# Attention's waits for tiles and banks: query turns in a projection bank, products moved ahead of a head's first turn, and the second key/value projection's banks in another order

## The chip, the cores and the metric

The kernel runs on one core of one Trainium2 chip. The metric is the device time of one execution in microseconds (us); less is better. Three runs of the kernel before gave 2050.15, 2051.71 and 2051.81 us, a median of 2051.71 us.

## The reference

One encoder layer is computed for two inputs of 512 tokens x 1024 channels, x_prompt (sample 0, s = 0 in the code) and x_sample (s = 1), with the same weights. Cut to what matters:

```python
x = x + 0.5 * swiglu(rms_norm(x, ffn1_norm), ffn1_w_gate, ffn1_w_up, ffn1_w_down)
h = rms_norm(x, mix_norm)
aq, ak, av, mq, mk, mv, gate_pre, o_pre, g_att, g_mlstm = split(h @ w_in)
aq = rope(rms_norm(heads(aq), q_norm))            # 8 query heads of 64
ak = rope(rms_norm(heads(ak), k_norm))            # 2 key/value heads
att = softmax(aq @ ak.T * 64 ** -0.5) @ av        # over all 512 keys
mem = mlstm_bidirectional(mq, mk, mv, gate_pre)   # 4 heads of 128, both directions
merged = sigmoid(g_att) * (att @ w_up_att) + sigmoid(g_mlstm) * (mem @ w_up_mlstm)
x = x + merged @ w_out
x = x + 0.5 * swiglu(rms_norm(x, ffn2_norm), ffn2_w_gate, ffn2_w_up, ffn2_w_down)
return rms_norm(x, final_norm)
```

Everything is float32, to float32 accuracy.

## The kernel before

**Precision.** A float32 operand is split into a rounded high part (written by ScalarE, L715) and the rest (VectorE, L716); a product is then three matmuls, high x high, high x rest, rest x high, summed in PSUM. In the profile they read `xh,w` and `xl,w`. Transposes are matmuls with the identity (`ident`).

**Order of the work.** Both samples' first feed-forward block, then for each sample `mix` (L840), a generator that holds the attention, the mLSTM and the merge, then the second feed-forward block. TensorE (PE) runs what is issued in program order where the code pins it (`pin`); VectorE (DVE) and ScalarE (ACT) are ordered by a scheduler, from the places of their instructions in the program and from what these wait for.

**PSUM.** It has eight banks of 128 x 512 floats. In `mix` they come from four pools, each of which hands its banks out in turn and makes the next user wait until the last reader of that bank is done: MM has three (tiles `mm`, for projections), PS two (`pss`, for scores), PT two (`pst`, for transposes), PO one (`pso`, for the products with the values).

**The projections of `mix`.** `tok_proj` (L783, matmuls on L800) computes keys, values and gates of all 512 tokens into four banks at once, 272 columns each: for each of eight slices of the weights, twelve products, three for each bank in turn. Its banks are listed by the caller: (PS, PS, MM, MM). In the second sample the merge of the first stands just ahead: `merge_mem` writes its last banks from PS and PT in turn, and VectorE reads each on L1218 (`scalar_tensor_tensor`). `proj` (L808) is a projection of 128 columns, 24 products into one bank of MM, that can be had as single steps (L820); its result is read by gates on ScalarE and VectorE.

**Gates.** `gates` (L948) sums the logarithms of the forget gates with two triangular matrices for each direction and with a matrix of ones (L970), products of 16 columns.

**Attention** (from L1150). A head h has four blocks b of 128 queries. `score(h, b)` makes a bank of scores (two products, L1091), VectorE takes the row maximum (L1094), ScalarE the exponential and its sum (L1096), VectorE the reciprocal (L1097), and the tile is scaled: on ScalarE (L1099) for odd b in the first sample, save head 0's last, else on VectorE (L1101). The values are wanted with the keys on the partitions, so `turn_keys(Ps, b)` (L1107) transposes 128 columns of **all four** tiles of a head into a bank of PT, and L715/L716 split it. `values` (L1118) multiplies the split tile of the turn before. So the loop of one (h, b) is: a query pair's turn, if it is due; score(h+1, b); five product steps of the projections; turn(h, b); three steps; values of the turn before. `among(n)` takes n such steps, out of a queue of projections for the attention gate and the output gate; they run out in head 6. Ahead of the loop the four scores of head 0 are made, with nine steps after each (`FIRST`).

The queries are turned in pairs of heads: `q_turn(pr)` (L1038) transposes four blocks into a bank of PT (`pair_turn`, L900), and four copies, two on ScalarE (L1041) and two on VectorE (L1042), take it to `qT`. Pair 0 is turned ahead of the loop, pairs 1 to 3 inside it, at h = 0, 2, 4 and b = 2.

Of the kernel before, what the change touches and what calls it, by code (L numbers as in the profile page):

```python
# [16 lines left out]
P = 128  # L17
# [9 lines left out]
def encoder(ctx, tc, I, outs):  # L27
    nc = tc.nc
# [13 lines left out]
    def nm(s):  # L42
        n_id[0] += 1
        return f"{s}_{n_id[0]}"
# [71 lines left out]
    def PT():  # L116
        return pt.tile([P, S], F32, tag="t", name=nm("pst"))

    def f(ap):
        return ap.bitcast(F32)  # L120
# [7 lines left out]
    ones = cpool.tile([P, P], F32, name="ones")  # L128
# [157 lines left out]
    def load_w(view, key, park=True):  # L286


        if key in parked:
            d, shape = parked[key]  # L290
            w2 = wpool.tile(shape, F32R, tag="w8", bufs=4, name=nm("w"))
            for i in range(2):
                nc.sync.dma_start(f(w2[:, i]), d[:, i])
            return w2[:, 0], w2[:, 1]
        raw = fetch_w(view)
        with shifted(-WEIGHTS):
            hi, lo = split_w(raw, V_)
        if not park:
            return hi, lo
        shape = [P, 2] + list(raw.shape[1:])  # L300
        parked[key] = d, _ = dpool.tile(shape, F32, name=nm("wpark")), shape
        for i, t in enumerate((hi, lo)):
            nc.sync.dma_start(d[:, i], f(t))
        return hi, lo
# [424 lines left out]
    tabs = []  # L729
# [41 lines left out]
    def go(*units):  # L771
        for load, comp in units:
            held.append((comp, load()))
            while len(held) > ahead[0]:
                c, w = held.pop(0)
                c(w)
# [6 lines left out]
    def tok_proj(xh, xl, cols, kk, done, banks):  # L783

        N = sum(n for _, n in cols)
        p = []

        def load(k0):
            return load_w([win_v[:, k0:k0 + kk, c:c + n] for c, n in cols], ("in", cols[0], k0))

        def comp(k0, w):
            wh, wl = w
            if not p:
                p.extend(b() for b in banks)
            for kl in range(kk):
                k = k0 + kl
                for b in range(4):
                    bs = slice(b * P, (b + 1) * P)
                    for i, (a, w_) in enumerate(((xh, wh), (xh, wl), (xl, wh))):
                        nc.tensor.matmul(p[b][:, :N], a[:, k, bs], w_[:, kl, :],  # L800
                                         start=(k == 0 and i == 0), stop=(k == KD - 1 and i == 2))
            if k0 + kk == KD:
                done(p)

        return [(lambda k0=k0: load(k0), lambda w, k0=k0: comp(k0, w)) for k0 in range(0, KD, kk)]
# [29 lines left out]

    OUT = 3
    FILLER = 5,3
    FIRST = 9

    def mix(s, xh, xl, early=None, extra=None, after=None):  # L840

# [8 lines left out]
        def F2(dtype=F32):  # L850
            return T2(dtype, "f2")
# [42 lines left out]
            yield tt(v, v, cg.unsqueeze(2).to_broadcast([P, 4, 2, DA]), op=ALU.mult)  # L894
            yield tt(v, v, m, op=ALU.add)

        def pair_turn(o, keep):
            p = PT()
            for b in range(4):
                keep(nc.tensor.transpose(p[:, b * P:(b + 1) * P], o[:, b, :], ident))  # L900
            return p
# [17 lines left out]
        qraw, rq = mg[:, 4:8, :], []  # L919
# [18 lines left out]
        def gs(tag):  # L938
            t = small(32, tag)
            return t, t.rearrange("p (d b h) -> p d b h", d=2, b=4)  # L940
# [7 lines left out]
        def gates():  # L948
            Gb = Gt.rearrange("p (b c) -> p b c", b=4)
            V_.tensor_tensor(Gb, Gb, gbias.unsqueeze(1).to_broadcast([P, 4, 16]), op=ALU.add)  # L950
            Gv = Gt.rearrange("p (b d g h) -> p b d g h", b=4, d=2, g=2)

            Fs, Fv = gs("Fs")
            Is, Iv = gs("Is")
            for dst, g in ((Fv, 1), (Iv, 0)):
                G_.tensor_copy(dst[:, 0], Gv[:, :, 0, g, :])
                for b in range(4):
                    G_.tensor_copy(dst[:, 1, 3 - b], Gv[:, b, 1, g, :])
            fa, _ = gs("fa")
            V_.scalar_tensor_tensor(fa, Fs, -1.0, Fs, op0=ALU.mult, op1=ALU.min)  # L960
            nc.scalar.activation(fa, fa, AF.Exp)
            nc.scalar.activation(fa, fa, AF.Ln, bias=1.0)
            nc.scalar.activation(warm, fa[:, 0:1], AF.Exp)
            Lt, _ = gs("Lt")
            V_.scalar_tensor_tensor(Lt, Fs, 0.0, fa, op0=ALU.min, op1=ALU.subtract)
            p = PT()
            for d in range(2):
                rhs = Lt[:, d * 16:(d + 1) * 16]
                for j, lhs in enumerate((tabs[2][:, 2 * d, :], tabs[2][:, 2 * d + 1, :], ones)):
                    nc.tensor.matmul(p[:, j * 32 + d * 16:j * 32 + (d + 1) * 16], lhs, rhs, start=True, stop=True)  # L970
            V_.tensor_copy(cs, p[:, 0:96])
            et, ev = gs("fa")
            V_.tensor_tensor(et, Is, cs[:, 32:64], op=ALU.add)
            p = PT()
            nc.tensor.transpose(p[0:32, 0:P], et, ident)
            rows = F2()[0:32]
            er, run = rows[:, 0:P], rows[:, P:2 * P]
            V_.tensor_copy(er, p[0:32, 0:P])
            nc.sync.dma_start(ebuf.rearrange("d b h s -> (d b h) s"), er)
            V_.tensor_tensor_scan(run[:, ::-1], er[:, ::-1], er[:, ::-1], NEG, op0=ALU.max, op1=ALU.max)  # L980
            V_.tensor_tensor_scan(run[0:16], er[0:16], er[0:16], NEG, op0=ALU.max, op1=ALU.max)
            top = rows[:, 2 * P:2 * P + 1]
            V_.tensor_reduce(top, er, axis=AX.X, op=ALU.max)
            return run, top

        def gate_tops(run, top):
            p = PT()
            pin(nc.tensor.transpose(p[:, 0:32], run, ident[0:32, 0:32]))
            pin(nc.tensor.transpose(p[:, 32:64], top.to_broadcast([32, P]), ident[0:32, 0:32]))
            V_.tensor_copy(st[:, 0:2], p[:, 0:64].rearrange("p (i d b h) -> p i d b h", i=2, d=2, b=4))  # L990
# [44 lines left out]
        def q_rope(pr):  # L1035
            return rope_steps(qraw[:, :, pr * P:(pr + 1) * P], rq[0][:, :, 2 * pr:2 * pr + 2], tabs[0])

        def q_turn(pr, keep):  # L1038
            p = pair_turn(qraw[:, :, pr * P:(pr + 1) * P], keep)
            for h, own, other in ((2 * pr, lower, upper), (2 * pr + 1, upper, lower)):  # L1040
                nc.scalar.activation(qT[own, h, :], p[own, :], AF.Copy)  # L1041
                V_.tensor_tensor(qT[other, h, :], p[own, :], f(qT[own, h, :]), op=ALU.subtract)  # L1042

        go(*tok_proj(xh, xl, [(512, 256), (2304, 16)], 2, kv_done, (PS, PS, MM, MM)))
        if early:
            early()
        go(*tok_proj(xh, xl, [(0, 512)], 2, q_done, (MM, PO, MM, MM)), mem_qk(0, 0), mem_qk(0, 1))
# [3 lines left out]
        with shifted(60):  # L1051
            k_turn()
            q_turn(0, lambda i: i)
# [82 lines left out]
        def among(n):  # L1136
            for _ in range(n):
                if not between:
                    if not held:
                        return  # L1140
                    c, w = held.pop(0)
                    if queue:
                        load, c2 = queue.pop(0)
                        held.append((c2, load()))
                    between.extend(c.steps(w))
                between.pop(0)()
# [6 lines left out]
        for b in range(4):  # L1153
            Ps.append(score(0, b))
            next(rope, None)
            among(FIRST)
        last = None
        for h in range(HA):
            nxt = []
            for b in range(4):  # L1160
                if h in (0, 2, 4) and b == 2:
                    q_turn(h // 2 + 1, pin)
                if (h, b) == (0, 1):
                    gate_tops(*tops)
                if (h, b) in ((0, 3), (2, 3)):
                    rope = q_rope(h // 2 + 2)
                if h < 4:
                    next(rope, None)
                if h + 1 < HA:
                    nxt.append(score(h + 1, b))  # L1170
                among(FILLER[0])
                pp = turn_keys(Ps, b)
                among(FILLER[1])
                if last:
                    values(*last)
                last = h, b, pp
                if extra and b == 2 and h in (2, 3, 4):
                    extra[h - 2]()
            Ps = nxt
# [320 lines left out]
    def keep(k, eng=None):  # L1500
        pin(keep_x(0, k, banks[k], x0r[k], eng))
# [156 lines left out]
    def mid_parts(s):  # L1658
# [10 lines left out]
        return one, two, three  # L1669

    m0 = mix(0, *nhl[0], None, mid_parts(1), prep1)
    for _ in range(3):
        next(m0)
# [182 lines left out]
```

## Time and profile before

| | |
|---|---|
| median of three runs | 2051.71 us (2050.15 to 2051.81) |
| the profiled execution's own time | 2048.82 us |
| its span | 2047.0 us |
| granted TensorE clock in it | 0.999 |
| instructions | 26767 |
| PE, matmuls (x9317) | 2033.1 us busy |
| VectorE (x2780) | 1571.5 us busy |
| ScalarE (x1655) | 909.0 us busy |
| GpSimd (x116) | 93.4 us busy |
| DMA | 445.38 MB, mean 218 GB/s |

The profile is that of one execution. A row of the timeline gives the start and the length in us, the engine, the line of the kernel, the operation, output tile <- input tiles, shape and type, and xN where N instructions alike stand together (the length is then from the first one's start to the last one's end). In brackets stands how long the engine had been idle before it and what ended that. PE's matmuls overlap: the next starts before the one ahead has ended, so PE's distance from start to start is shorter than the length of one. The waits of PE give, for each kind of instruction, what it waited for: us in total, times, longest.

### The profile page before, as it was taken

The numbers are of one execution on the slowest core, as the hardware profiler recorded it, in microseconds if no ns is written. First come the engines' busy times: TensorE is split into PE (matmuls) and PEld (weight loads), VectorE is DVE, ScalarE is ACT, GpSimd is POOL, SyncE is SP. The second block draws the span as 40 slices with busy tenths as digits, with TensorE's granted clock in tenths as the row PEclk, the third lists the DMA queues.
The fourth block names the chain that finished last, engine by engine and source line by source line (L and its number), as shares of the span: only waits on it lengthen the run. The fifth ranks groups of instructions, "written<-read, shape, count | busy, mean of one in ns | idle before, by whom it ended". The sixth has DMA issues, their size and how long they took to land.

```text
span 2047.0 us, 26767 instructions
## 1 busy us (share of the span) xinstructions
PE 2033.1 (99%) x9317; PEld 1679.9 (82%) x9317; DVE 1571.5 (77%) x2780; ACT 909.0 (44%) x1655; POOL 93.4 (5%) x116
## 2 busy tenths in 40 slices
PE   9999999999999999999999999999999999999998
PEld 7888888888888878888888888888888888888887
DVE  8888888886797888776567756366788988786797
ACT  7544444443234567563324554134544444442224
POOL 0000000001003000100120000001000000000001
PEclk9999999999999999999999999999999999999999
DMA  9656566799766853868564345667655655599753
GB/s 316 199 168 226 174 203 194 240 339 357 262 224 225 292 164 128 286 212 289 187 190 137 117 150 174 221 202 228 193 186 184 197 175 183 198 345 347 272 200 119
DMA packets 314727, 445.38 MB, mean 218 GB/s; under 512 B 19848, under 2 KB 189920, under 8 KB 313312
## 3 DMA queue, kind: packets, MB, share of 16 engines
q1 hardware_dynamic: 312512, 437.69, 63.8%
q0 software_dynamic: 1920, 5.72, 0.9%
q8 instruction: 73, 1.20, 0.2%
q14 instruction: 62, 0.51, 0.1%
q10 hardware_dynamic: 160, 0.27, 0.0%
HBM read 284.06 MB, written 159.55 MB: 217 GB/s over the span
## 4 chain that ended last, share of the span: by engine, by line
PE 95%; DVE 3%; ACT 1%; DMA 0%; issue 0%; SPq 0%; DVEq 0%; ACTq 0%
PE mm L833 16%; PE pst L374 12%; PE pso L374 12%; PE mm L374 11%; PE mm L632 8%; PE pss L374 6%; PE pst L632 4%; PE pss L632 4%; PE mm L820 4%; PE mm L800 4%; PE pso L632 3%; PE pso L1118 1%; PE pst L1107 1%; PE pss L1091 1%; PE pso L1287 1%; PE pss L1237 1%
## 5 line engine op out<-in xcount | busy, mean ns | idle before, releaser
L374 PE MATMUL pst<-xc,w 128*128 128x512 f32 x1056 | 253.7, 389 | 0.0
L374 PEld LDWEIGHTS pst<-xc,w 128*128 128x128 f32 x1056 | 198.3, 188 | 41.1
L374 PE MATMUL mm<-xc,w 128*128 128x512 f32 x972 | 229.4, 390 | 0.0
L374 PEld LDWEIGHTS mm<-xc,w 128*128 128x128 f32 x972 | 182.0, 188 | 37.7 <-ACT f L382 0.2
L632 PE MATMUL mm<-rt,w 128*128 128x512 f32 x765 | 178.7, 389 | 0.0
L833 PE MATMUL mm<-xh,w 128*128 128x512 f32 x560 | 176.9, 392 | 0.0
L632 PEld LDWEIGHTS mm<-rt,w 128*128 128x128 f32 x765 | 143.5, 188 | 29.7
L332 ACT ACTIVATE w<-t 128x512 fp32r<-128x512 f32 x176 | 106.6, 627 | 135.5 <-issue 63.1
L333 DVE TENSOR_TENSOR w<-t,w 128x512 fp32r<-128x512 f32 x176 | 117.8, 688 | 42.5 <-ACT w L332 41.0
L374 PE MATMUL pso<-xc,f 128*128 128x512 f32 x528 | 126.8, 389 | 0.0
L374 PE MATMUL pss<-xc,w 128*128 128x512 f32 x528 | 126.8, 389 | 0.0
L374 PE MATMUL pso<-xc,w 128*128 128x512 f32 x528 | 126.8, 389 | 0.0
L833 PEld LDWEIGHTS mm<-xh,w 128*128 128x128 f32 x560 | 104.9, 188 | 21.8
L374 PEld LDWEIGHTS pss<-xc,w 128*128 128x128 f32 x528 | 99.1, 188 | 20.6
L374 PEld LDWEIGHTS pso<-xc,w 128*128 128x128 f32 x528 | 99.1, 188 | 20.5
L374 PEld LDWEIGHTS pso<-xc,f 128*128 128x128 f32 x528 | 99.1, 188 | 20.6
L820 PE MATMUL mm<-xh,w 128*128 128x512 f32 x336 | 114.5, 401 | 0.0
L833 PE MATMUL mm<-xl,w 128*128 128x512 f32 x280 | 109.6, 391 | 0.0
L715 ACT ACTIVATE w<-wr 128x512 fp32r<-128x512 f32 x72 | 45.1, 632 | 136.7 <-PE pso L632 70.7
L278 ACT ACTIVATE w<-wr 128x1024 fp32r<-128x1024 f32 (+1 forms) x64 | 65.3, 1029 | 80.5 <-issue 23.7
L279 DVE TENSOR_TENSOR w<-wr,w 128x1024 fp32r<-128x1024 f32 (+1 forms) x64 | 79.8, 1248 | 27.7 <-ACT w L278 16.8
L715 ACT ACTIVATE w<-t 128x512 fp32r<-128x512 f32 x82 | 51.8, 632 | 107.6 <-PE pst L632 62.4
(440 smaller groups left out, 4067.0 us busy)
## 6 DMA issues: line engine op xcount, KB each, us to landing
rt<-rbuf SPq DMA_DIRECT2D x154, 512.0 KB, 5.7
wpark<-w SPq DMA_DIRECT2D x88, 512.0 KB, 3.5
w<-wpark SPq DMA_DIRECT2D x88, 512.0 KB, 4.5
wr<-in_ffn_w_gate_dram SPq DMA_DIRECT2D x62, 512.0 KB, 5.4
rbuf<-tab SPq DMA_DIRECT2D x102, 256.0 KB, 4.0
wr<-in_ffn_w_up_dram SPq DMA_DIRECT2D x44, 512.0 KB, 4.5
rbuf<-f SPq DMA_DIRECT2D x72, 256.0 KB, 4.0
wr<-in_w_in_dram SPq DMA_DIRECT2D x36, 512.0 KB, 5.6
```

What stands on the lines that cost most here:

```text
L278: pin(nc.scalar.activation(hi, raw, AF.Copy))
L279: pin(lo_eng.tensor_tensor(lo, raw, f(hi), op=ALU.subtract))
L332: pin(nc.scalar.activation(t[:, 0], src, AF.Copy))
L333: pin(V_.tensor_tensor(t[:, 1], src, f(t[:, 0]), op=ALU.subtract))
L374: nc.tensor.matmul(p, a[:, k, :], xt[:, b, k, :], start=(first and k == 0 and i == 0), stop=(k == HK_ - 1 and i == 2), skip_group_check=True)
L632: nc.tensor.matmul(p, u[:, a, d * P:(d + 1) * P], r[:, b, ts], start=(first and q == 0 and k == 0), stop=(q == len(us) - 1 and k == 2), sk ...
L715: nc.scalar.activation(hi, src, AF.Copy)
L800: nc.tensor.matmul(p[b][:, :N], a[:, k, bs], w_[:, kl, :], start=(k == 0 and i == 0), stop=(k == KD - 1 and i == 2))
L820: pin(nc.tensor.matmul(p[0], a[:, k, :], b, start=(k == 0 and i == 0), stop=(k == n - 1 and i == 2)))
L833: nc.tensor.matmul(p, a[:, k, :], b, start=(k == 0 and i == 0), stop=(k == n - 1 and i == 2))
L1091: pin(nc.tensor.matmul(p, qT[:, h, b * P:(b + 1) * P], kv[:, hk * 2 + j, :], start=(j == 0), stop=(j == 1)))
L1107: pin(nc.tensor.transpose(p[:, b * P:(b + 1) * P], Ps[b][:, kb * P:(kb + 1) * P], ident))
```

## The change

Five edits, all in `mix`. `FIRST` gives the steps after each of head 0's scores one by one, 7, 9, 9 and 11 in place of four times 9. `SOON` puts seven steps ahead of a head's first turn and one behind it, in place of five and three; the other turns keep `FILLER`. Query pairs 1 to 3 are turned in a bank of MM; pair 0 stays in PT. In `gates` the two products with ones become one of 32 columns. The second sample's keys and values go to the banks (PS, MM, MM, PS).

```diff
     FILLER = 5,3
-    FIRST = 9
+    SOON = 7,1
+    FIRST = 7,9,9,11
...
-        def pair_turn(o, keep):
-            p = PT()
+        def pair_turn(o, keep, bank=PT):
+            p = bank()
...
-                for j, lhs in enumerate((tabs[2][:, 2 * d, :], tabs[2][:, 2 * d + 1, :], ones)):
-                    nc.tensor.matmul(p[:, j * 32 + d * 16:j * 32 + (d + 1) * 16], lhs, rhs, start=True, stop=True)
+                for j in range(2):
+                    nc.tensor.matmul(p[:, j * 32 + d * 16:j * 32 + (d + 1) * 16], tabs[2][:, 2 * d + j, :], rhs,
+                                     start=True, stop=True)
+            nc.tensor.matmul(p[:, 64:96], ones, Lt, start=True, stop=True)
...
-            p = pair_turn(qraw[:, :, pr * P:(pr + 1) * P], keep)
+            p = pair_turn(qraw[:, :, pr * P:(pr + 1) * P], keep, MM if pr else PT)
...
-        go(*tok_proj(xh, xl, [(512, 256), (2304, 16)], 2, kv_done, (PS, PS, MM, MM)))
+        go(*tok_proj(xh, xl, [(512, 256), (2304, 16)], 2, kv_done, (PS, MM, MM, PS) if s else (PS, PS, MM, MM)))
...
-            among(FIRST)
+            among(FIRST[b])
...
-                among(FILLER[0])
+                n0, n1_ = FILLER if b else SOON
+                among(n0)
                 pp = turn_keys(Ps, b)
-                among(FILLER[1])
+                among(n1_)
```

The changed kernel's lines lie one to four further down. First place: PE at the first turn of head 3 in the first sample (the name is the tile, its numbers count tiles; `t2` are the four probability tiles, `mm` is a projection's bank). Before:

```order
L1091 MATMUL pss_581_6379<-kv_361_5275,qT_364_5278 128x512 x2
L820 MATMUL mm_569_6329<-xh_329_4894,w_542_6213 128x512
L820 MATMUL mm_569_6329<-xl_330_4895,w_542_6213 128x512
L820 MATMUL mm_569_6329<-xh_329_4894,w_542_6213 128x512 x2
L820 MATMUL mm_569_6329<-xl_330_4895,w_542_6213 128x512
L1107 MATMUL pst_584_6393<-ident_87,t2_550_6240 128x128
L1107 MATMUL pst_584_6393<-ident_87,t2_557_6273 128x128
L1107 MATMUL pst_584_6393<-ident_87,t2_565_6311 128x128
L1107 MATMUL pst_584_6393<-ident_87,t2_577_6355 128x128
L820 MATMUL mm_569_6329<-xh_329_4894,w_542_6213 128x512 x2
L820 MATMUL mm_569_6329<-xl_330_4895,w_542_6213 128x512
L1118 MATMUL pso_561_6294<-t2_579_6369,kv_361_5275 128x512
```

And in the changed kernel:

```order
L820 MATMUL mm_569_6328<-xh_329_4894,w_542_6212 128x512
L820 MATMUL mm_569_6328<-xl_330_4895,w_542_6212 128x512
L820 MATMUL mm_569_6328<-xh_329_4894,w_542_6212 128x512 x2
L820 MATMUL mm_569_6328<-xl_330_4895,w_542_6212 128x512
L820 MATMUL mm_569_6328<-xh_329_4894,w_542_6212 128x512 x2
L1110 MATMUL pst_584_6394<-ident_87,t2_550_6239 128x128
L1110 MATMUL pst_584_6394<-ident_87,t2_557_6272 128x128
L1110 MATMUL pst_584_6394<-ident_87,t2_565_6310 128x128
L1110 MATMUL pst_584_6394<-ident_87,t2_577_6354 128x128
L820 MATMUL mm_569_6328<-xl_330_4895,w_542_6212 128x512
L1121 MATMUL pso_561_6293<-t2_579_6368,kv_361_5275 128x512
```

Two products stand ahead of the four transposes that stood behind them: seven and one, in place of five and three.

Second place: ScalarE around the same turn (`t_577` is the last of the four tiles that the turn needs, `t_583` a tile of the next head, `t_579` and `t_585` splits of turned tiles). Before:

```order
L1096 ACTIVATE t_577_6355,asm_6353<-pss_6350,asm_6353 128x512
L715 ACTIVATE t_579_6369<-pst_6364 128x512
L1096 ACTIVATE t_583_6384,asm_6382<-pss_6379,asm_6382 128x512
L1099 ACTIVATE t_577_6355<-t_577_6355,asm_6353 128x512
L715 ACTIVATE t_585_6398<-pst_6393 128x512
```

And in the changed kernel:

```order
L1099 ACTIVATE t_577_6354,asm_6352<-pss_6349,asm_6352 128x512
L715 ACTIVATE t_579_6368<-pst_6363 128x512
L1102 ACTIVATE t_577_6354<-t_577_6354,asm_6352 128x512
L1099 ACTIVATE t_583_6383,asm_6381<-pss_6378,asm_6381 128x512
L715 ACTIVATE t_585_6399<-pst_6394 128x512
```

The scale of the tile that the turn needs (L1099 before, L1102 now) stands ahead of the next head's exponential (L1096 before, L1099 now), not behind it.

Third place: PE at the turn of query pair 2. Before and in the changed kernel:

```order
L1118 MATMUL pso_561_6294<-t2_552_6254,kv_361_5275 128x512
L1118 MATMUL pso_561_6294<-t2_553_6255,kv_361_5275 128x512
L900 MATMUL pst_562_6297<-ident_87,mg_365_5279 128x128 x4
L1091 MATMUL pss_563_6306<-kv_361_5275,qT_364_5278 128x512 x2
L820 MATMUL mm_544_6219<-xh_329_4894,w_517_6110 128x512 x2
```

```order
L1121 MATMUL pso_561_6293<-t2_552_6255,kv_361_5275 128x512
L1121 MATMUL pso_561_6293<-t2_553_6256,kv_361_5275 128x512
L901 MATMUL mm_562_6296<-ident_87,mg_365_5279 128x128 x4
L1094 MATMUL pss_563_6305<-kv_361_5275,qT_364_5278 128x512 x2
L820 MATMUL mm_544_6218<-xh_329_4894,w_517_6109 128x512 x2
```

The four transposes stand in the same place and write a bank of MM (`mm`) in place of one of PT (`pst`). On GpSimd and SyncE the order is the same before and after.

## The prediction

> **What bounds the kernel now.** I read the page first: the span, the busy shares and the chain that ended last.
>
> ```profile
> span 2047.0 us, 26767 instructions
> PE 2033.1 (99%) x9317; PEld 1679.9 (82%) x9317; DVE 1571.5 (77%) x2780; ACT 909.0 (44%) x1655; POOL 93.4 (5%) x116
> PE 95%; DVE 3%; ACT 1%; DMA 0%; issue 0%; SPq 0%; DVEq 0%; ACTq 0%
> ```
>
> TensorE is busy for 99% of the span and carries 95% of the chain. A change can save only products, or the few places where PE stands still. So the second view is the waits of PE, of which five rows lie in what the change touches (total, times, longest, in us):
>
> ```profile
> PE pst L1107 <- DVE t L716: 1.0, 2, 0.7
> PE pss L800 <- DVE t L1218: 0.8, 1, 0.8
> PE pst L1107 <- ACT t L1099: 0.7, 1, 0.7
> PE pst L1107 <- DVE t L1101: 0.6, 1, 0.6
> PE pst L1107 <- DVE qT L1042: 0.3, 1, 0.3
> ```
>
> Six waits, 3.4 us by this view. It counts from the modelled end of a matmul; what PE loses is larger, since products overlap. I therefore take each stall as start to next start, less the usual distance. For a 512-wide product that is 0.23 us, from two neighbours in the third view, the timeline:
>
> ```profile
> 756.06 0.39 PE L820 MATMUL mm<-xh,w 128*128 128x512 f32 x1
> 756.29 0.40 PE L820 MATMUL mm<-xl,w 128*128 128x512 f32 x1
> ```
>
> Four 128x128 transposes take 0.60 us to the last end and three 0.49 us (rows below), so one follows another after 0.11 us.
>
> **The change part by part.** All times are from the profiled execution, whose own time is 2048.82 us, 1.8 us over its span and 2.9 us under the median of the three timed runs, 2051.71 us. Savings are worked out in the span and taken off both.
>
> *Two products ahead of a head's first turn (SOON, FIRST).* The first turn of a head transposes all four probability tiles, so it waits for the scale of the newest. Two of these waits show. Place A is head 0 of the first sample:
>
> ```profile
> 716.52 0.49 PE L1107 MATMUL pst<-ident,t 128*128 128x128 f32 x3
> 717.02 0.48 DVE L1101 TENSOR_SCALAR t<-t,asm 128x512 f32<-128x512 f32 x1
> 717.56 0.33 PE L1107 MATMUL pst<-ident,t 128*128 128x128 f32 x1 [0.55 <-DVE t L1101]
> ```
>
> The fourth transpose was due at 716.52 + 3 x 0.11 = 716.85 and started at 717.56: 0.71 us lost. With two more products ahead (0.45 us) PE gets there at 717.30. FIRST also moves the fourth score two products earlier, but VectorE, on which its maximum stands in line, has nothing free there (9.86 of 10 us in the window that holds place A, third figure after the window's length being DVE):
>
> ```profile
> 710.00:720.00 10.00, 9.45 (x44) 7.38 (x43) 9.86 (x24) 5.39 (x12) 0.00 (x0) 1.00 0.79 237
> ```
>
> I leave the scale's end where it is: 0.26 us of stall stays, **0.45 us** saved. If the earlier score did help, all 0.71 would go.
>
> Place C is head 3:
>
> ```profile
> 756.45 0.59 ACT L715 ACTIVATE t<-pst 128x512 fp32r<-128x512 f32 x1
> 756.87 0.15 DVE L1097 RECIPROCAL asm<-asm 128x1 f32<-128x1 f32 x1
> 756.99 0.69 ACT L1096 ACTIVATE t<-pss,asm 128x512 f32<-128x512 f32 x1
> 757.21 0.49 PE L1107 MATMUL pst<-ident,t 128*128 128x128 f32 x3
> 757.66 0.71 ACT L1099 ACTIVATE t<-t,asm 128x512 f32<-128x512 f32 x1
> 758.43 0.33 PE L1107 MATMUL pst<-ident,t 128*128 128x128 f32 x1 [0.72 <-ACT t L1099]
> ```
>
> The fourth transpose was due at 757.54 and started at 758.43: 0.89 us lost. Its scale, ready from 757.02 (the reciprocal's end), stood behind the next tile's exponential on ScalarE. In the changed order the scale comes first: it can start when L715 ends, at 757.04, ends at 757.75, and the transpose follows at 757.81, by the 0.06 us that lie between scale and transpose above. PE arrives at 757.54 again (0.45 later by the two products, 0.45 earlier by place B), so 0.27 stays and **0.62 us** go. The exponential that is passed ends 0.7 us later, at about 758.4; its tile is wanted only at the next head's first turn, four turns on (the turns of B and C above stand 3.2 us apart, so some 13 us).
>
> What is added is that the two products no longer stand behind the turn, where they cover its split before the products with the values. The tightest of these is head 1 of the first sample:
>
> ```profile
> 733.57 0.68 DVE L716 TENSOR_TENSOR t<-pst,t 128x512 fp32r<-128x512 f32 x1
> 734.99 0.63 PE L1118 MATMUL pso<-t,kv 128*128 128x512 f32 x2
> ```
>
> The rest is done at 734.25, the product that reads it starts at 735.22 (one product into the pair). Of 0.97 us of slack 0.45 go. So this edit costs **nothing** by this trace, unless VectorE runs 0.53 us later there.
>
> *Query turns in a projection bank.* The turn of place B waited for the transposes' bank that the query pair still held:
>
> ```profile
> 748.26 0.60 PE L900 MATMUL pst<-ident,mg 128*128 128x128 f32 x4
> 753.13 0.69 DVE L1042 TENSOR_TENSOR qT<-pst,qT 64x512 fp32r<-64x512 f32 x1
> 753.29 0.39 PE L820 MATMUL mm<-xh,w 128*128 128x512 f32 x1
> 753.97 0.63 PE L1107 MATMUL pst<-ident,t 128*128 128x128 f32 x4 [0.29 <-DVE qT L1042]
> ```
>
> Due 753.52, started 753.97: **0.45 us**, all of it saved. At D and F the turn waited for the other bank, since with the query pair in one of two, turns follow each other in the one that is left:
>
> ```profile
> 777.72 0.68 DVE L716 TENSOR_TENSOR t<-pst,t 128x512 fp32r<-128x512 f32 x1
> 777.84 0.40 PE L820 MATMUL mm<-xl,w 128*128 128x512 f32 x1
> 778.55 0.63 PE L1107 MATMUL pst<-ident,t 128*128 128x128 f32 x4 [0.31 <-DVE t L716]
> ```
> ```profile
> 1097.36 0.40 PE L820 MATMUL mm<-xh,w 128*128 128x512 f32 x1
> 1097.63 0.68 DVE L716 TENSOR_TENSOR t<-pst,t 128x512 fp32r<-128x512 f32 x1
> 1098.46 0.63 PE L1107 MATMUL pst<-ident,t 128*128 128x128 f32 x4 [0.71 <-DVE t L716]
> ```
>
> Due 778.07 and 1097.59: **0.48 and 0.87 us**, both saved, since those turns then take a bank free since the turn before last. The price is a projection bank held from 748.26 to 753.82. There are three; a projection fills one with 24 products, and the held bank comes up again only after two others, 48 products or at least 10.9 us. No wait between nothing and 5.6 us fits in there; I take nothing.
>
> *Second sample's key/value banks.* Place E is the start of that projection:
>
> ```profile
> 982.23 0.28 PE L800 MATMUL pss<-w,xl 128*128 128x272 f32 x1
> 982.55 0.68 DVE L1218 SCALAR_TENSOR_TENSOR t<-t,pss 128x512 f32<-128x512 f32 x1
> 983.28 0.52 PE L800 MATMUL pss<-w,xh 128*128 128x272 f32 x2 [0.77 <-DVE t L1218]
> 983.76 0.41 PE L800 MATMUL mm<-w,xh 128*128 128x272 f32 x2
> L864 DVE TENSOR_TENSOR t<-mm,R x1: 692/692/692, 960.4 to 960.4; 128x512 f32<-128x512 f32 x1
> ```
>
> One product takes 0.41 - 0.28 = 0.13 us to the next. The second bank, due 982.36, was released at 983.28: 0.92 us lost. Now six products into two projection banks, last read at 960.4 + 0.69 = 961.1, run first: 6 x 0.125 = **0.75 us** saved, and 0.17 us of the wait stays. The two banks' order for the copies behind changes too, by at most the six products; they lie beside the query projection.
>
> *Gates.* Two 128x16 products with ones become one of 128x32; each product is two instructions in the trace.
>
> ```profile
> 686.43 0.38 PE L970 MATMUL pst<-Lt,ones 128*128 128x16 f32 x2
> 686.66 0.60 PE L970 MATMUL pst<-Lt,tab 128*128 128x16 f32 x4
> L970 PE MATMUL pst<-Lt,ones x8: 262/263/263, 686.4 to 1034.3; 128*128 128x16 f32 x8
> ```
>
> Such a pair holds PE for 0.23 us. The wider one isn't in the trace: 128x16 instructions stand 0.115 us apart and 128x128 ones 0.11, so 32 columns cost the same, between nothing and 0.01 us more. **0.23 us** in the second sample; in the first, PE only reaches place A earlier and waits there for VectorE, so nothing.
>
> The Trainium skill, "TensorE: Matmul & The Clock Gate", section "Back-to-back issue gap", has about 60 cycles or 25 ns for 1 to 64 columns. By that the second sample's two instructions would bring 0.05 us, and the sum would be 0.18 us smaller; the trace disagrees, at 0.115 us each.
>
> **The sum:** 0.45 (A) + 0.45 (B) + 0.62 (C) + 0.48 (D) + 0.75 (E) + 0.87 (F) + 0.23 = 3.85 us. Span 2043.15, profiled execution 2044.97; against the median, 2051.71 - 3.85 = **2047.9 us**, 0.19% faster. A measurement of this kernel tells about 0.2%, 4.1 us, from no change, so this lies just within.
>
> **The rivals.**
>
> *All six stalls go.* If VectorE and ScalarE, which wait for PE at many scores, move forward with it, the rests at A, C and E vanish too, and both gates count: 0.71 + 0.45 + 0.89 + 0.48 + 0.92 + 0.87 + 0.46 = 4.78 us, 2046.9 us. For it: ScalarE's chain at C hangs on a turn that itself starts 0.45 earlier by B. Against it: VectorE at 9.86 of 10 us at A.
>
> *Only the bank waits go.* If VectorE sets when probabilities and the merge end, PE arrives sooner and waits the same time later: A, C and E bring nothing, B, D, F and one gate 2.03 us: 2049.7 us. For it: the same window. Against it: C's delay is an order on ScalarE that has changed.
>
> *The rests come late (slower).* With one product instead of three behind a first turn, the products with the values could wait for VectorE's rest at L716, wherever that ends late by over 0.53 us (head 1) to some 2 us (most heads). Fourteen first turns have such products, seven heads in two samples (the projections run out in the seventh); each could lose 0.45 us, 6.3 in all, against the 2.03 us of the bank waits: +4.3 us, 2056.0 us. Against it: even the tightest place has 0.52 us left after the edit.
>
> **How the numbers follow.** My sum gets 0.45, all stalls 0.27, only banks 0.19, slower 0.09. The three runs of before span 1.66 us, so a true 3.85 measures beyond 4.1 a little under half the time (0.20 of the 0.45) and a true 4.78 three times in four (0.20): faster 0.40. Slower takes two thirds of its rival and a little of the third case: 0.08. The rest, 0.52, is within. The range goes from the second case less the spread of the runs (2046.9 - 1.6 = 2045.3) to the banks-only case plus half of it, 2050.5; the slower rival stays out.
>
> **What would show it.** After the change the waits of PE have no row with qT L1042 and none of a turn on L716; the key/value row is at 0.2 or gone; the scale rows at 0.3 or gone. If a wait of the values' products on L716 appears, the last rival is at work; if the waits on the scales and on the merge stay as long as they were, banks-only. A wait of a projection's first product on the query copies would make the free bank wrong. Any lower granted clock would void the sum.

## The result, and the profile after

Fifteen runs of each kernel give a median of 2045.78 us for the changed one (2044.33 to 2048.44) and 2050.34 us for the one before (2048.41 to 2051.81). The ratio is 0.9979, with a 95% interval of 0.9972 to 0.9987: faster by 0.21%, between 0.13% and 0.28%. That lies on the bound that the prediction set for "within".

The page of the changed kernel (span, busy shares, share of the chain):

```profile
span 2043.0 us, 26753 instructions
PE 2032.5 (99%) x9313; PEld 1679.4 (82%) x9313; DVE 1570.5 (77%) x2780; ACT 908.6 (44%) x1655; POOL 94.3 (5%) x116
PE 97%; DVE 2%; DMA 1%; ACT 0%; issue 0%; SPq 0%; DVEq 0%; ACTq 0%
```

The span is 4.0 us shorter. Its waits of PE, in full (total, times, longest):

```profile
PE pst L1350 <- DVE xc L1432: 1.6, 1, 1.6
PE mm L1480 <- ACT w L1443: 0.6, 1, 0.6
PE pst L1370 <- DMA raw<-in_x_prompt_dram: 0.5, 2, 0.3
PE mm L1480 <- ACT xc L1463: 0.5, 1, 0.5
```

All five rows that the change was about are gone from this view, and what is left lies at the program's start and in the feed-forward stages. The view is coarse, though: it counts from the modelled end of a matmul, and leaves short waits out. What is left at the places shows in the timeline, by the distance from start to start. Place A first:

```profile
715.83 0.94 PE L1110 MATMUL pst<-ident,t 128*128 128x128 f32 x4
715.90 0.48 DVE L1104 TENSOR_SCALAR t<-t,asm 128x512 f32<-128x512 f32 x1
716.43 0.14 PEld L1110 LDWEIGHTS pst<-ident,t 128*128 128x128 f32 x1 [0.35 <-DVE t L1104]
```

Four transposes take 0.94 us, not 0.60: the fourth was due at 716.16, but its weights (the scaled tile) could be loaded at 716.43 only, when VectorE's scale had ended (715.90 + 0.48). 0.28 us are left of 0.71. Place C:

```profile
755.20 0.59 ACT L715 ACTIVATE t<-pst 128x512 fp32r<-128x512 f32 x1
755.67 0.72 ACT L1102 ACTIVATE t<-t,asm 128x512 f32<-128x512 f32 x1
755.97 0.81 PE L1110 MATMUL pst<-ident,t 128*128 128x128 f32 x4
756.29 0.69 ACT L1099 ACTIVATE t<-pss,asm 128x512 f32<-128x512 f32 x1
```

The scale now runs ahead of the exponential, and PE loses 0.15 us in place of 0.89. At B and F (the product ahead of the turn, then the turn) nothing is lost, and the same at D; a turn follows 0.23 us behind:

```profile
752.01 0.39 PE L820 MATMUL mm<-xh,w 128*128 128x512 f32 x1
752.24 0.60 PE L1110 MATMUL pst<-ident,t 128*128 128x128 f32 x4
...
1093.60 0.39 PE L820 MATMUL mm<-xh,w 128*128 128x512 f32 x1
1093.83 0.60 PE L1110 MATMUL pst<-ident,t 128*128 128x128 f32 x4
```

At E the second bank of PS, now the fourth, is due at 980.38 and is let go by VectorE at 980.49: the product starts at 980.54, 0.16 us late in place of 0.92.

```profile
979.81 0.68 DVE L1222 SCALAR_TENSOR_TENSOR t<-t,pss 128x512 f32<-128x512 f32 x1
980.25 0.28 PE L800 MATMUL mm<-w,xl 128*128 128x272 f32 x1
980.54 0.52 PE L800 MATMUL pss<-w,xh 128*128 128x272 f32 x2
```

And one place is new. At head 1 of the first sample, the first product with the values comes late; VectorE's rows are shown with PE's:

```profile
730.06 1.23 DVE L279 TENSOR_TENSOR w<-wr,w 128x1024 fp32r<-128x1024 f32 x1
731.28 0.67 DVE L1097 TENSOR_REDUCE asm<-pss 128x1 f32<-128x512 f32 x1
731.87 0.48 DVE L1104 TENSOR_SCALAR t<-t,asm 128x512 f32<-128x512 f32 x1
732.26 0.68 DVE L716 TENSOR_TENSOR t<-pst,t 128x512 fp32r<-128x512 f32 x1
732.87 0.67 DVE L1133 TENSOR_TENSOR f<-pso,f 64x512 f32<-64x512 f32 x1
733.05 0.40 PE L820 MATMUL mm<-xh,w 128*128 128x512 f32 x1
733.59 0.30 PEld L1121 LDWEIGHTS pso<-t,kv 128*128 128x128 f32 x2 [0.59 <-DVE f L1133]
733.60 0.73 PE L1121 MATMUL pso<-t,kv 128*128 128x512 f32 x2
```

The products with the values of head 1 go into the one bank of PO, which head 0's result still holds until VectorE has copied it (L1133, to 733.54). PE was due at 733.28 and starts at 733.60: 0.32 us. In the trace of before the same stretch of VectorE reads:

```profile
732.42 1.23 DVE L279 TENSOR_TENSOR w<-wr,w 128x1024 fp32r<-128x1024 f32 x1
733.57 0.68 DVE L716 TENSOR_TENSOR t<-pst,t 128x512 fp32r<-128x512 f32 x1
734.17 0.67 DVE L1130 TENSOR_TENSOR f<-pso,f 64x512 f32<-64x512 f32 x1
734.77 0.67 DVE L1094 TENSOR_REDUCE asm<-pss 128x1 f32<-128x512 f32 x1
```

There a row maximum (L1094, in the changed kernel L1097) stood behind the copy. Now that maximum, counted along its line the same one, stands ahead of it (731.28), though the scale behind it (731.87) is no newcomer: it stood ahead of the copy before too, at 731.52. VectorE's order has changed at a place that the diff doesn't touch. Before, the copy ended at 734.84, 0.15 us ahead of the product at 734.99.

**Where the time went.** The start of one and the same product in the two traces, before less after, grows along the mixing stage by these steps:

| step | us |
|---|---|
| gates, first sample | 0.22 |
| A | 0.44 |
| the turn behind the first query pair | 0.11 |
| head 1, the bank of PO | -0.42 |
| B | 0.43 |
| C | 0.73 |
| D | 0.48 |
| E | 0.76 |
| gates, second sample | 0.22 |
| F | 0.88 |
| sum | 3.85 |

(At head 1 the first product is 0.32 us late, and the second starts 0.33 us behind it, at 733.93, where two such products usually stand 0.23 apart: 0.42 in all.) The whole stage, from its first key/value product to its last projection product, took 1402.74 - 646.63 = 756.11 us before and 1398.25 - 645.75 = 752.50 after:

```profile
646.63 0.41 PE L800 MATMUL pss<-w,xh 128*128 128x272 f32 x2
1402.74 0.39 PE L833 MATMUL mm<-mh,w 128*128 128x512 f32 x1
```
```profile
645.75 0.41 PE L800 MATMUL pss<-w,xh 128*128 128x272 f32 x2
1398.25 0.39 PE L833 MATMUL mm<-mh,w 128*128 128x512 f32 x1
```

So the stage is 3.61 us shorter; the other 0.24 us went in steps of some 0.05 us along the stage. The 0.4 us that the span gained beyond that lie outside the stage: 0.88 ahead of the stage, where PE waited 1.4 us for the first input's DMA before and 0.5 in this execution, less 0.49 behind it.

### The profile page after: what moved, and what is told of

Same layout as the page of the kernel before. It is cut to its first block, busy times and chain, and to the rows that moved or that the text cites. A ratio compares the mean times of both kernels' runs of the same rounds, so it can differ in the third digit from the quotient of the medians.

```text
span 2043.0 us, 26753 instructions
## 1 busy us (share of the span) xinstructions
PE 2032.5 (99%) x9313; PEld 1679.4 (82%) x9313; DVE 1570.5 (77%) x2780; ACT 908.6 (44%) x1655; POOL 94.3 (5%) x116
## 4 chain that ended last, share of the span: by engine, by line
PE 97%; DVE 2%; DMA 1%; ACT 0%; issue 0%; SPq 0%; DVEq 0%; ACTq 0%
PE mm L833 16%; PE pst L374 12%; PE pso L374 12%; PE mm L374 11%; PE mm L632 8%; PE pss L374 6%; PE mm L820 5%; PE pst L632 4%; PE pss L632 4%; PE mm L800 4%; PE pso L632 3%; PE pso L1121 1%; PE pss L1094 1%; PE pst L1110 1%; PE pso L1291 1%; PE pss L1241 1%
```

## The experiments

A stall below is a distance from start to start, less the usual one; "stage" is by how much the length that was just defined is shorter than before.

**Three parts alone.** First the bank of the query turns alone.

```diff
-        def pair_turn(o, keep):
-            p = PT()
+        def pair_turn(o, keep, bank=PT):
+            p = bank()
...
-            p = pair_turn(qraw[:, :, pr * P:(pr + 1) * P], keep)
+            p = pair_turn(qraw[:, :, pr * P:(pr + 1) * P], keep, MM if pr else PT)
```

> Only query pairs 1 to 3 are turned in a projection bank; all else as before. Both theories: the stalls B (0.45 us), D (0.48) and F (0.87) go, no projection waits for the query copies, A stays at 0.71 and the order on ScalarE at head 3 is that of before. Theory 1 (the prediction's: VectorE and ScalarE end where they ended, PE only arrives sooner): the 0.45 us of B come back at C, whose stall grows from 0.89 to about 1.34 us; sum 1.35 us, ratio 0.9993. Theory 2 (the softmax chain hangs on PE's scores and moves with it): C stays at 0.89 or less; sum 1.80 us, ratio 0.9991.

B, D and F went, A stayed at 0.72, no projection waited, and C grew to 1.30 us (due 756.54). Ratio 0.9988 (0.9979 to 0.9996); stage 1.41 us. The timeline at C, ScalarE and PE:

```profile
756.40 0.69 ACT L1096 ACTIVATE t<-pss,asm 128x512 f32<-128x512 f32 x1
757.06 0.72 ACT L1099 ACTIVATE t<-t,asm 128x512 f32<-128x512 f32 x1
757.84 0.33 PE L1107 MATMUL pst<-ident,t 128*128 128x128 f32 x1 [1.13 <-ACT t L1099]
```

The scale is behind the exponential as before, and its end did not come nearer: of the 0.45 us of B, 0.41 are given back four microseconds on. That is theory 1. At head 1 the copy ended 0.27 us ahead of the product: no wait there.

Then the steps around the first turns alone.

```diff
-    FIRST = 9
+    SOON = 7,1
+    FIRST = 7,9,9,11
...
-            among(FIRST)
+            among(FIRST[b])
...
-                among(FILLER[0])
+                n0, n1_ = FILLER if b else SOON
+                among(n0)
                 pp = turn_keys(Ps, b)
-                among(FILLER[1])
+                among(n1_)
```

> Only the steps around the first turns (FIRST and SOON); banks and gates as before. B, D and F stay (0.45, 0.48, 0.87). A falls from 0.71 to about 0.27. At C PE arrives 0.45 later than in the changed kernel, since B stays, so the 0.15 left there should go: C 0.89 saved. Theory 1 (the new 0.43 us at the first values products of head 1 are the bank of PO, which VectorE's copy of head 0's result still held, and come with SOON alone): 0.43 lost there; sum 0.44 + 0.89 - 0.43 = 0.90 us, ratio 0.9996. Theory 2 (they come from the bank edit, which moved VectorE's work there): nothing lost at head 1; sum 1.33 us, ratio 0.9994.

A fell to 0.28, C went altogether, B, D and F stayed at 0.48, 0.48 and 0.88, and at head 1 nothing was lost. So theory 1's reason for head 1 fell: it doesn't come with these steps alone. But by the run ahead it doesn't come with the banks alone either. The stage was only 0.15 us shorter, since 0.63 us more were lost in the second sample's mLSTM, where VectorE waited 0.55 us for a DMA (more on that below), and the rest in smaller waits of the first's. Ratio 0.9994 (0.9985 to 1.0003), no difference that can be told.

Then the key/value banks and the gates alone.

```diff
-                for j, lhs in enumerate((tabs[2][:, 2 * d, :], tabs[2][:, 2 * d + 1, :], ones)):
-                    nc.tensor.matmul(p[:, j * 32 + d * 16:j * 32 + (d + 1) * 16], lhs, rhs, start=True, stop=True)
+                for j in range(2):
+                    nc.tensor.matmul(p[:, j * 32 + d * 16:j * 32 + (d + 1) * 16], tabs[2][:, 2 * d + j, :], rhs,
+                                     start=True, stop=True)
+            nc.tensor.matmul(p[:, 64:96], ones, Lt, start=True, stop=True)
...
-        go(*tok_proj(xh, xl, [(512, 256), (2304, 16)], 2, kv_done, (PS, PS, MM, MM)))
+        go(*tok_proj(xh, xl, [(512, 256), (2304, 16)], 2, kv_done, (PS, MM, MM, PS) if s else (PS, PS, MM, MM)))
```

> Only the second key/value projection's banks and the gates' products; attention as before. E falls from 0.92 to 0.17 us, 0.22 us less at the gates of each sample. Theory 1 (the prediction's: VectorE sets place A, so the first sample's 0.22 us are given back): A grows from 0.71 to 0.93; sum 0.75 + 0.22 = 0.97 us, ratio 0.9995. Theory 2 (VectorE's chain moves with PE): A stays at 0.71; sum 1.19 us, ratio 0.9994. B, C, D, F as before.

E fell to 0.16, the gates gave 0.22 us in each sample, and A stayed at 0.71. PE's rows at A:

```profile
716.80 0.49 PE L1109 MATMUL pst<-ident,t 128*128 128x128 f32 x3
717.83 0.33 PE L1109 MATMUL pst<-ident,t 128*128 128x128 f32 x1 [0.54 <-DVE t L1103]
```

Due at 717.13, started 717.83. That is theory 2: what PE saves 30 us ahead, VectorE follows, though the trace of before has it busy for 9.86 of 10 us there. Stage 1.18 us; ratio 0.9990 (0.9981 to 0.9999). Here too head 1 loses nothing, and in the traces of all three parts the maximum stands behind the copy, as before. So it takes more than one of the three parts to move it; which of them together was not run.

**Head 1.** First its two products were put back.

```diff
-                n0, n1_ = FILLER if b else SOON
+                n0, n1_ = FILLER if b or h == 1 else SOON
```

> The changed kernel, but head 1's first turn keeps five steps ahead and three behind. Theory 1 (PE waited at head 1 for the bank of PO, and the two products gave the copy its time): the 0.32 + 0.11 us there are gone, and nothing else changes: stalls 0.28 at A, 0.15 at C, 0.17 at E; about 0.43 us faster than the changed kernel, ratio to before 0.9976 where that had 0.9979. Theory 2 (VectorE is late there whatever PE does): a wait of about 0.3 us stays at head 1, and the ratio is that of the changed kernel.

The stall stayed, 0.30 us. Theory 1 was wrong, and it could have been seen: the values of a first turn are multiplied behind the second turn, and eight steps lie in between whichever way they are split. Theory 2, that VectorE is late, was left. Ratio 0.9977 (0.9968 to 0.9986), as the changed kernel's. So next VectorE's order:

```diff
-            V_.tensor_tensor(af[o0:o0 + DA, :], po[o0:o0 + DA, :], t[o0:o0 + DA, :], op=ALU.add)
+            with shifted(-10 if h == 0 and not s else 0):
+                V_.tensor_tensor(af[o0:o0 + DA, :], po[o0:o0 + DA, :], t[o0:o0 + DA, :], op=ALU.add)
```

> The changed kernel with VectorE's copy of head 0's result in the first sample one place earlier, ahead of the rest of the second turned tile. Theory 1 (the order on VectorE, in which the next head's row maximum now stands ahead of the copy that frees the bank of PO, makes PE wait at head 1): the copy ends 0.6 us earlier, 0.3 us before PE comes, and the 0.32 + 0.11 us are gone; ratio 0.9977 where the changed kernel had 0.9979. Theory 2 (the products wait for the rest of the turned tile as much as for the bank): the wait only moves to the second product, 0.3 us stay.

```profile
734.05 0.68 DVE L1134 TENSOR_TENSOR f<-pso,f 64x512 f32<-64x512 f32 x1
734.65 0.67 DVE L716 TENSOR_TENSOR t<-pst,t 128x512 fp32r<-128x512 f32 x1
734.99 0.89 PE L1121 MATMUL pso<-t,kv 128*128 128x512 f32 x2
735.38 0.19 PEld L1121 LDWEIGHTS pso<-t,kv 128*128 128x128 f32 x1 [0.41 <-DVE t L716]
735.43 0.19 DVE L1077 TENSOR_TENSOR st<-cs,st 128x32 f32<-128x32 f32 x1
```

The copy ends 0.25 us ahead of the product, and the first product is on time: the bank was what PE waited for. But the second product now waits for the rest of the turned tile, made behind the copy: 0.17 us stay. Half of theory 1, half of theory 2; the stage is 0.28 us shorter than the changed kernel's, which is less than two traces of the changed kernel differ by (0.35, below), and the ratio, 0.9978 (0.9968 to 0.9987), can't tell. The maximum still stood ahead of both: with it there, neither order of copy and rest is in time. Putting the maximum behind both, as it stood before, was not run. Instead, one piece of its work was given to GpSimd, the rest of one weight slice:

```diff
-            hi, lo = split_w(raw, V_)
+            hi, lo = split_w(raw, G_ if key == ("in", 2320) else V_)
```

> The changed kernel with the rest of one weight slice (the output gate's first, in the first sample, 1.23 us on VectorE ahead of place head 1) made by GpSimd; the row maximum still stands ahead of the copy on VectorE. Theory 1 (VectorE is simply behind at head 1: split, maximum, rest and copy in a row, and any of them taken away ends the wait): the copy ends over 0.4 us earlier against PE, and both products of the values are on time: 0 us in place of 0.32, some 0.4 us gained. Theory 2 (the maximum's place ahead of the copy alone makes the wait): 0.3 us stay.

Neither came in the one run of this kernel. The stall grew to 2.18 us. The timeline, GpSimd (POOL), VectorE and PE:

```profile
730.97 2.40 POOL L279 TENSOR_TENSOR w<-wr,w 128x1024 fp32r<-128x1024 f32 x1 [69.12 <-DVE st L1076]
731.01 2.42 DVE L1077 TENSOR_TENSOR st<-cs,st 128x32 f32<-128x32 f32 x1
735.59 0.67 DVE L1133 TENSOR_TENSOR f<-pso,f 64x512 f32<-64x512 f32 x1
736.32 0.73 PE L1121 MATMUL pso<-t,kv 128*128 128x512 f32 x2 [2.01 <-DVE f L1133]
```

A VectorE instruction that takes 0.19 us elsewhere (L1077 above) took 2.42, exactly while GpSimd ran. As a test of the theories the run is spoilt, but it shows the chain with a larger sign: VectorE some 2.2 us late ahead of the copy makes PE 1.9 us later (2.18 in place of 0.32).

**Places A and C.** The next three kernels were timed once each, so only their traces are read. First the steps behind head 0's scores.

```diff
-    FIRST = 7,9,9,11
+    FIRST = 9,9,9,9
```

> The changed kernel with nine steps after each of head 0's scores, so the fourth score comes two products later again; SOON stays. Theory 1 (the prediction's: VectorE has nothing free ahead of place A, so the earlier score does nothing): A stays at 0.28 us. Theory 2 (the earlier score is what brought the scale forward): A grows by up to 0.45, to 0.5 to 0.73 us. Elsewhere as in the changed kernel: C 0.15, E 0.17, 0.32 + 0.11 at head 1.

A was 0.26, all else as in the changed kernel; stage 3.62 us. Theory 1: this edit does nothing, VectorE takes the earlier score no sooner. Then C's two parts, from both sides: the changed kernel with head 3's products put back, and the kernel before with nothing but these two products moved.

```diff
-                n0, n1_ = FILLER if b else SOON
+                n0, n1_ = FILLER if b or h == 3 else SOON
```

> The changed kernel, but head 3's first turns keep five steps ahead and three behind; ScalarE's order at place C is that of the changed kernel. Theory 1 (the order is worth about 0.7 us, the two products 0.45): C is 0.15 + 0.45 = 0.60 us, where with the old order and the banks alone it was 1.30. Theory 2 (only the products count): C is about 1.30 us.

```profile
757.16 0.49 PE L1110 MATMUL pst<-ident,t 128*128 128x128 f32 x3
758.14 0.33 PE L1110 MATMUL pst<-ident,t 128*128 128x128 f32 x1 [0.48 <-ACT t L1102]
```

```diff
+    SOON = 7,1
...
-                among(FILLER[0])
+                n0, n1_ = FILLER if b or h != 3 or s else SOON
+                among(n0)
                 pp = turn_keys(Ps, b)
-                among(FILLER[1])
+                among(n1_)
```

> The kernel before with seven steps ahead of head 3's first turn and one behind in the first sample alone; ScalarE's order at place C is that of before. Theory 1 (the scale ends where it did, the products fill the wait): C falls from 0.89 to 0.44 us, the other places stay. Theory 2 (the chain moves with PE's place): C stays at 0.89.

```profile
759.35 0.49 PE L1108 MATMUL pst<-ident,t 128*128 128x128 f32 x3
760.11 0.33 PE L1108 MATMUL pst<-ident,t 128*128 128x128 f32 x1 [0.27 <-ACT t L1100]
```

With the order alone C is 0.65 us (758.14 less 757.49), with the products alone 0.43 (760.11 less 759.68). Theory 1 in both: the scale's new place on ScalarE is worth 1.30 - 0.65 = 0.65 us, the two products 0.89 - 0.43 = 0.46. The second of these kernels lost 1.0 us more than before in the second sample's mLSTM, behind a DMA that landed late:

```profile
1230.27 0.69 DVE L1065 TENSOR_TENSOR box<-box,tab 128x512 f32<-128x512 f32 x1 [0.94 <-DMA box<-ebuf]
1231.84 0.73 PE L1239 MATMUL pss<-qk,qk 128*128 128x512 f32 x2 [0.99 <-DVE t L1255]
```

This wait came in two of the thirteen traces (this one and that of the first turns' steps alone); the DMA had been issued 6.6 us ahead of PE's due start in both, as in the trace of before. What makes it late there stays open.

**All that was left, and the changed kernel again.** Eight steps ahead of the turn at heads 0 and 3, the copy first as above, and E's last bank from PO:

```diff
-                n0, n1_ = FILLER if b else SOON
+                n0, n1_ = FILLER if b else (8, 0) if h in (0, 3) and not s else SOON
...
-        go(*tok_proj(xh, xl, [(512, 256), (2304, 16)], 2, kv_done, (PS, MM, MM, PS) if s else (PS, PS, MM, MM)))
+        go(*tok_proj(xh, xl, [(512, 256), (2304, 16)], 2, kv_done, (PS, MM, MM, PO) if s else (PS, PS, MM, MM)))
...
-        go(*tok_proj(xh, xl, [(0, 512)], 2, q_done, (MM, PO, MM, MM)), mem_qk(0, 0), mem_qk(0, 1))
+        go(*tok_proj(xh, xl, [(0, 512)], 2, q_done, (MM, PS, MM, MM) if s else (MM, PO, MM, MM)), mem_qk(0, 0), mem_qk(0, 1))
```

> The changed kernel with what is left of its stalls filled: eight steps ahead of the first turn (none behind) at heads 0 and 3 of the first sample, the copy of head 0's result one place earlier on VectorE, and the second sample's key/value banks (PS, MM, MM, PO), its query banks (MM, PS, MM, MM). Theory 1 (the ends of the chains at A and C stay where they are, one product more is 0.23 us less): A 0.28 to 0.05, C 0.15 to nothing, E 0.16 to nothing, head 1 0.32 to 0.17; 0.7 us less than the changed kernel, ratio to before 0.9976 where that has 0.9979. Theory 2 (another order on VectorE gives it back elsewhere): single stalls go, but new ones of the same size come, and the sum of the stalls in the mixing stage stays within 0.2 us of the changed kernel's.

> The changed kernel a second time, beside the combined one on the same chip, for its time and for how far two traces of one kernel agree. Both theories: the same stalls, A 0.28, C 0.15, E 0.16, head 1 0.32, each within 0.03 us, and a ratio of 0.9979 within its interval; waits on DMA at the start of the kernel may differ by several tenths.

A, C and E are gone from the combined kernel's trace. Head 1 has 0.35 us, on the second product, and a new stall of 0.42 stands in the first sample's mLSTM, in the waits of PE as

```profile
PE pst L1284 <- DVE row L240: 0.3, 1, 0.3
```

So theory 2 holds in good part. Its stage is 3.81 us shorter than before; that of the changed kernel's second trace 3.26, with A 0.28, C 0.16, E 0.17 and head 1 0.31 again, and 0.35 us of other small waits. The ratios, 0.9973 (0.9962 to 0.9984) and 0.9977 (0.9967 to 0.9986), don't tell the two apart. There is no version here that is shown to beat the changed kernel.

## Why the prediction was right, point by point

It forecast 3.85 us less; the medians say 4.56 (2050.34 - 2045.78), between 2.7 and 5.7 by the interval, the steps in the trace 3.85. The absolute time was forecast 2.1 us too high, mostly because the median of three runs stood 1.4 us above that of fifteen. That the steps add up to the very sum is luck: against it stand 0.42 us lost at head 1, which the sum had at nothing, and 0.43 us gained that it had not counted (0.21 at the gates, 0.11 at C, 0.11 at a place of its own).

- **A, 0.45:** measured 0.44. VectorE had no use for the earlier score, as the run with nine steps shows.
- **B, D and F, 0.45, 0.48 and 0.87:** measured 0.43, 0.48 and 0.88. The projection bank never made anything wait, neither in the changed kernel nor alone. A seventh small place of this kind, in the first sample, gave 0.11 more.
- **C, 0.62:** measured 0.73. Both parts were right, the order and the products; the scale ended a little sooner than I put it.
- **E, 0.75:** measured 0.76; 0.16 left where 0.17 was forecast.
- **Gates, 0.23 in one sample:** measured 0.22 in both. The step "in the first, PE only reaches place A earlier and waits there for VectorE, so nothing" is wrong: with the gates alone A did not grow. With the banks alone, C did, by 0.41 of the 0.45 us that B had saved. So one scale's end stayed where it was against a saving of 4 us ahead, and another's followed one of 30 us ahead. I had taken "VectorE is 9.86 of 10 us busy" for "nothing can come earlier": with the gates' edit it is busy for 9.87 of the same 10 us, and yet came earlier. Why it could is not shown.
- **"So this edit costs nothing by this trace, unless VectorE runs 0.53 us later there":** 0.42 us were lost at that very head. I had looked at the slack of one thing that the products need, the rest of their tile. That slack shrank much as forecast: the rest was done at 732.94, 0.57 us ahead of 733.51, where the second product was due, against 0.52 in the prediction. The other, the bank of PO, had 0.15 us of slack before, in a row that was in the trace. And the prediction looks at the orders on PE and ScalarE, not at VectorE's, where a maximum had moved ahead of the copy. That the bank was what the first product waited for is shown, by the run with the copy first; that the maximum made the copy late is argued, from the order alone: it stands ahead of the copy in all eight traces that have all parts of the change, and behind it in the other five, none of which has the stall. None of the three parts moves it alone.

The rivals: that all six stalls go is refuted by 0.28, 0.15 and 0.16 us at A, C and E; that only the bank waits go, by A, C and E too. The slower one had the right engine and the right head, but PE lost 0.4 us once, not fourteen times, and at a bank. When the copy was put first, its own mechanism, the late rest, did appear, with 0.17 us.

## What to carry to other kernels

Where a tuned kernel's bounding engine is 99% busy, take every stall as start to next start, and price an edit by the row that ends it. Here the places priced so came out within 0.11 us each, and the larger misses, 0.21 and 0.42 us, lay in places put at nothing. For each thing that is moved ask what else the waiting instruction needs, banks above all, and compare the orders of all engines, since a scheduler may move work where the diff doesn't. And ask how far ahead a saving lies: in the one case of each kind here, the chain behind followed a saving of 30 us ahead, and one of 4 us ahead was given back at the next wait.

## What the runs showed of the hardware that was not expected

GpSimd kept VectorE out. A 128x32 addition on VectorE took 2.42 us in place of 0.19, beginning 0.04 us behind a GpSimd subtraction of 2.40 us and ending 0.06 us behind its end. Work that is moved from VectorE to GpSimd to relieve it can so cost VectorE more than it took, here 2.2 us for 1.23. The Trainium skill, "SBUF — State Buffer", section "SBUF: two separate sides", has the rule: the two share a pair of ports by an exclusive lock, which whoever starts first holds for its whole instruction, and a VectorE instruction with two inputs from SBUF needs it. These rows agree. So does the other side in the changed kernel's trace: a VectorE instruction with one input in PSUM (`xs<-pss,xs`, 626.83) took its usual 0.68 us in the middle of a GpSimd instruction of 1.29 us that had begun at 626.79.

Two traces of one kernel agree to 0.02 us at the four stalls named, while its stage differs by 0.35 us and the start of the kernel by 1.9 us (645.75 and 647.64 at the stage's first product).
